# Order of the second-phase products and of the combining in a seven-product matmul block

## The chip, the cores and the metric

The kernel runs on one core of one Trainium2 chip. The metric is the device time of one execution in microseconds (us), as the median of several runs. The core has four engines that matter here, each with its own queue of instructions: TensorE (PE) multiplies, VectorE (DVE) and ScalarE (ACT) do elementwise work, and GpSimd (POOL) and SyncE (SP) issue DMA transfers here.

## What is computed

The reference is a two-layer decoder trunk over 256 tokens of width 2048 in float32. The change lies in the last line of each layer, the gated feed-forward part of width 5632:

```python
for l in range(DEPTH):
    ...
    x = x + mixed @ w_out[l]
    h2 = rms_norm(x, norm2_g[l])
    x = x + (jax.nn.silu(h2 @ w_gate[l]) * (h2 @ w_up[l])) @ w_down[l]
```

## The kernel before

**Tiles.** The 256 tokens are two halves of 128. A weight tile is 256 rows by 512 columns, loaded as 128 x 1024 by one DMA of 512 KB (`raw_load`, L81, seven buffers, issued by SP in program order). Float32 weights are multiplied as a sum of two parts: `split2` (L88) casts the tile on ScalarE to `wh` (L94, five buffers) and subtracts on VectorE to get the rest, `wl` (L95, four buffers). `mm3` (L123) then issues three matmuls of 512 columns: L124 with wh, L125 with wl, L126 with wh again. An ordinary tile (`unit`, L128) takes 12 matmuls, a tile of a seven-product block (`s_unit`, L566) takes 6.

**The feed-forward part.** Its 5632 columns are 11 blocks of 512. For block 0 of each layer, `gate_up` (L646) computes gate and up in the ordinary way. For the ten others, `seven` (L563) takes gate and up of both token halves as a 2 x 2 by 2 x 2 block product, with seven block products in place of eight. The tokens' halves give the left blocks, even and odd groups of rows of the gate and up weights the right ones: B11 and B21 from w_gate, B12 and B22 from w_up.

A seven-product block has two phases, and five PSUM banks (`bank[0]` to `bank[4]`, tiles named m, the pool `pa` with five buffers):

- In the first phase, L583 to L603, each of four steps loads B11, B12 and B22, forms three sums of them on VectorE (L591, L592, L595), and issues five products, into banks 0, 1, 3, 4 and 2. The sum B11 + B12 + B22, tile t2, is used in a product, then a DMA issued by POOL adds B21 to it in place (L597), and it is kept for later.
- Then the banks are combined: m0 is bank 0 plus bank 3 (L607 on ScalarE, L608 on VectorE), c21 is bank 2 plus m0 (L609) and is copied back into bank 2 (L610, ScalarE), c12 is bank 1 plus m0 (L611) plus bank 4 (L613), c22 is bank 1 plus c21 (L612).
- In the second phase, L615 to L622, the four B21 tiles are multiplied into bank 0 and the four kept tiles into bank 2. Banks 0 and 2 then hold the gate of the two token halves, c12 and c22 their up values with the sign turned.
- Last, L623 to L628: silu of banks 0 and 2 on ScalarE (L625), the product with c12 and c22 on VectorE (L627), and `act_later` (L555), which has the result transposed.

**Transposes.** `act_T` (L539) transposes the gated result on TensorE into a PSUM tile `ps_f` of which there is one buffer, casts it on ScalarE (L543) and subtracts on VectorE (L544), to give a pair of tiles aT for the down projection.

**Order.** The seven-product blocks and the ordinary tiles (gate and up of block 0, and all down projections, `std_stream`) are two generators; each `yield` of a seven-product block lets the ordinary stream issue so many tiles that both end together. A clock counts issued tiles (`tick`, L107: 1 for an ordinary tile, 0.5 for a product of a seven-product block), and `later(delay, fn)` (L104) runs a function when the clock has gone on by `delay`. `act_later` asks for the two transposes 2 and 3 ticks later. The framework then puts the instructions of each engine into an order of its own, by the dependences; that order is fixed in the built program. The seam, below, is the place where one seven-product block ends and the next begins.

Of the kernel before, what the change touches and what calls it, by code (L numbers as in the profile page):

```python
# [15 lines left out]
AF = mybir.ActivationFunctionType  # L16
ALU = mybir.AluOpType
# [46 lines left out]
def trunk(ctx, tc, x, xt, w_in, w_out, w_gate, w_up, w_down, sgu_w, sgu_g, consts,  # L64
          band, out):
    nc = tc.nc
# [14 lines left out]
    def raw_load(src, parts=1):  # L81
        raw = wp.tile([P, 2, NB], F32, tag="raw", name="raw", bufs=7)
        n = 2 // parts
        for i in range(parts):
            nc.sync.dma_start(raw[:, i * n : (i + 1) * n, :], src[:, i * n : (i + 1) * n, :])
        return raw

    def split2(raw):  # L88
        wh = wp.tile([P, 2, NB], F32R, tag="wh", name="wh", bufs=5)
        wl = wp.tile([P, 2, NB], F32R, tag="wl", name="wl", bufs=4)  # L90
        step = 2 if clock[0] > 1 else 1
        for j in range(0, 2, step):
            src = raw[:, j : j + step, :]
            nc.scalar.copy(wh[:, j : j + step, :], src)  # L94
            nc.vector.tensor_tensor(  # L95
                wl[:, j : j + step, :], src, f(wh[:, j : j + step, :]), ALU.subtract
            )
        return wh, wl
# [5 lines left out]
    def later(delay, fn):  # L104
        pending.append((clock[0] + delay, next(serial), fn))

    def tick(w=1.0):  # L107
        clock[0] += w
        due = sorted((e for e in pending if e[0] <= clock[0]), key=lambda e: e[:2])
        pending[:] = [e for e in pending if e[0] > clock[0]]  # L110
        for e in due:
            e[2]()
# [10 lines left out]
    def mm3(acc, ah, al, wh, wl, first, last, again=False):  # L123
        nc.tensor.matmul(acc, ah, wh, start=first, stop=False, skip_group_check=again)  # L124
        nc.tensor.matmul(acc, ah, wl, start=False, stop=False, skip_group_check=again)  # L125
        nc.tensor.matmul(acc, al, wh, start=False, stop=last, skip_group_check=again)  # L126
# [70 lines left out]
    def finish_rms(ss, width):  # L197
        tot = small([P, NTOK], "tot")
        nc.vector.tensor_reduce(tot, ss, AX.X, ALU.add)
        r = inv_rms(tot, NTOK, width)  # L200
        return [r[:, t : t + 1] for t in range(NTOK)]
# [38 lines left out]
    for lay in range(L):  # L240
# [287 lines left out]
        rstd2 = finish_rms(ss2, D)  # L528
# [4 lines left out]
        nrstd2 = [nr[:, t : t + 1] for t in range(NTOK)]  # L533
# [16 lines left out]
        def release(live=live, held=held, act_T=act_T):  # L550
            while held and live[0] < ACT_TILES:
                live[0] += 1
                act_T(*held.pop(0))

        def act_later(b, sg, held=held, release=release):  # L555
            for c in range(2):
                def ready(c=c):
                    held.append((b, c, sg))
                    release()

                later(2 + c, ready)

        def seven(b, lay=lay, pairs2=pairs2, ext2=ext2, act_later=act_later):  # L563
            bank = [pa.tile([P, NB], F32, tag="acc", name=f"m{i}") for i in range(5)]

            def s_unit(raw, m, i, op, first, last, bank=bank):  # L566
                wh, wl = split2(raw)
                for j in range(2):
                    ah, al = (op(2 * i + j, h) for h in range(2))
                    mm3(  # L570
                        bank[m], ah, al, wh[:, j, :], wl[:, j, :], first and j == 0,
                        last and j == 1, m in (0, 2),
                    )
                tick(0.5)

            def a_op(k, t):
                return lambda p, h: pairs2[p][:, h, k, t * P : (t + 1) * P]

            def e_op(n):
                return lambda p, h: ext2[p][:, h, n, :]  # L580

            kept = []
            for i in range(4):  # L583
                b11 = raw_load(w_gate[lay, b, i, 0])
                b12 = raw_load(w_up[lay, b, i, 0])
                b22 = raw_load(w_up[lay, b, i, 1])
                t2 = ap.tile([P, 2, NB], F32, tag="spt", name="t2", bufs=4)
                first, last = i == 0, i == 3
                s_unit(b11, 0, i, a_op(0, 0), first, last)
                yield  # L590
                nc.vector.tensor_tensor(b11, b11, b12, ALU.add)  # L591
                nc.vector.tensor_tensor(t2, b11, b22, ALU.add)  # L592
                s_unit(b11, 1, i, e_op(1), first, last)
                yield
                nc.vector.tensor_tensor(b12, b12, b22, ALU.add)  # L595
                s_unit(t2, 3, i, e_op(2), first, last)
                nc.gpsimd.dma_start(t2, w_gate[lay, b, i, 1], accum_op=ALU.add)  # L597
                yield
                s_unit(b22, 4, i, e_op(3), first, last)
                yield  # L600
                s_unit(b12, 2, i, e_op(0), first, last)
                yield
                kept.append(t2)  # L603
            m0, c12, c21, c22 = (
                zp.tile([P, NB], F32, tag="z", name=v) for v in ("m0", "c12", "c21", "c22")
            )
            nc.scalar.copy(m0, bank[0])  # L607
            nc.vector.tensor_tensor(m0, bank[3], m0, ALU.add)  # L608
            nc.vector.tensor_tensor(c21, bank[2], m0, ALU.add)  # L609
            nc.scalar.copy(bank[2], c21)  # L610
            nc.vector.tensor_tensor(c12, bank[1], m0, ALU.add)  # L611
            nc.vector.tensor_tensor(c22, bank[1], c21, ALU.add)  # L612
            nc.vector.tensor_tensor(c12, bank[4], c12, ALU.add)  # L613
            yield
            for i in range(5):  # L615
                if i < 4:
                    b21 = raw_load(w_gate[lay, b, i, 1])
                    s_unit(b21, 0, i, a_op(1, 0), False, i == 3)
                    yield
                if i > 0:  # L620
                    s_unit(kept[i - 1], 2, i - 1, a_op(1, 1), False, i == 4)
                    yield  # L622
            sg = [m0, c21]  # L623
            for t, c in ((0, bank[0]), (1, bank[2])):
                nc.scalar.activation(sg[t], c, AF.Silu, scale=rstd2[t])  # L625
            for t, c in ((0, c12), (1, c22)):
                nc.vector.scalar_tensor_tensor(sg[t], c, nrstd2[t], sg[t], ALU.mult, ALU.mult)  # L627
            act_later(b, sg)  # L628
            yield

        seven_done = [False]
# [1 line left out]
        def s_stream(seven=seven):  # L633
            for b in S_BLOCKS:
                yield from seven(b)
# [171 lines left out]
```

## Time and profile before

| | |
|---|---|
| runs of the kernel (3) | 1949.12 to 1950.69 us, median 1949.98 |
| profiled execution | 1948.9 us |
| its span, first to last instruction | 1947.2 us |
| mean granted TensorE clock | 0.998 |
| matmuls | 8836 |
| read from HBM | 422.66 MB, 218 GB/s over the span |

Rows of groups of instructions give the line, engine, operation, output and input tiles and shapes, the count, busy time and mean duration. Rows of a timeline begin with the start in us from the span's start and the duration, and end in brackets with the idle time of the engine before them and what ended it. Rows of waits give who waited for whom: us in total, how often, and the longest. Rows of stretches (A:B) give their length, the busy time and count of PE, PEld (weight loads of TensorE), DVE, ACT and POOL, the granted clock of TensorE, the busy share of the DMA engines and GB/s. Matmuls are pipelined: the row of one lasts 0.39 us, while in a dense stretch they start 0.227 us apart.

### The profile page before, as it was taken

How to read it: one execution, taken by the hardware profiler on the slowest of the kernel's cores; microseconds unless marked ns; L12 is line 12 of the kernel's file. 1: busy time of each engine (PE TensorE's matmuls, PEld its weight loads, DVE VectorE, ACT ScalarE, POOL GpSimd, SP SyncE). 2: the span in 40 equal slices, each digit the busy share in tenths (PEclk: the TensorE clock that was granted, in tenths of full speed). 3: DMA queues.
4: the chain of work that ended last, by engine and by line, in shares of the span. 5: the costliest groups of instructions: out<-in, count | busy, mean ns of one | idle time of the engine just before them, and what ended most of it. 6: DMA issues, size and time to landing. Idle time of an engine off the chain costs nothing.

```text
span 1947.2 us, 25055 instructions
## 1 busy us (share of the span) xinstructions
PE 1929.0 (99%) x8836; PEld 1577.2 (81%) x8836; DVE 1657.5 (85%) x1752; ACT 1304.9 (67%) x1729; POOL 122.1 (6%) x124
## 2 busy tenths in 40 slices
PE   9999999999999999999999999999999999999999
PEld 7788887878888888888887888878788888888887
DVE  6666689999999999999556666899999999999993
ACT  7566566667767776777756755666677677767675
POOL 1210000000000000000002000000000000000000
PEclk9999999999999999999999999999999999999999
DMA  9544557667777787778555345576678777876783
GB/s 368 190 146 152 185 173 238 219 217 245 253 214 242 243 265 221 236 227 273 195 203 191 126 170 176 174 247 226 201 243 263 222 241 226 271 216 237 237 264 124
DMA packets 118958, 426.41 MB, mean 219 GB/s; under 512 B 13232, under 2 KB 13872, under 8 KB 118832
## 3 DMA queue, kind: packets, MB, share of 16 engines
q1 hardware_dynamic: 105264, 375.52, 53.1%
q0 software_dynamic: 13568, 49.29, 13.6%
q8 instruction: 69, 1.13, 0.2%
q14 instruction: 57, 0.47, 0.1%
HBM read 422.66 MB, written 2.10 MB: 218 GB/s over the span
## 4 chain that ended last, share of the span: by engine, by line
PE 91%; issue 3%; DVE 3%; ACT 2%; POOL 1%; DMA 1%; SPq 0%; ACTq 0%; DVEq 0%; POOLq 0%
PE m L125 13%; PE m L124 13%; PE m L126 13%; PE acc L125 8%; PE acc L126 8%; PE acc L124 8%; PE dacc L124 8%; PE dacc L125 8%; PE dacc L126 8%; PE ps_f L188 1%; DVE wl L95 1%; POOL ir L171 1%; PE ps_v L361 1%; ACT wh L94 1%; PE ps_n L188 1%
## 5 line engine op out<-in xcount | busy, mean ns | idle before, releaser
L94 ACT CAST wh<-raw 128x1024 fp32r<-128x1024 f32 (+1 forms) x786 | 804.2, 1049 | 443.4 <-DVE raw L591 178.0
L95 DVE TENSOR_TENSOR wl<-raw,wh 128x1024 fp32r<-128x1024 f32 (+1 forms) x786 | 934.2, 1218 | 170.9 <-PE acc L125 92.7
L125 PE MATMUL m<-wl,ext 128*128 128x512 f32 x640 | 253.0, 395 | 0.3 <-DVE wl L95 0.2
L124 PE MATMUL m<-wh,ext 128*128 128x512 f32 x640 | 251.8, 395 | 0.7 <-ACT wh L94 0.7
L126 PE MATMUL m<-wh,ext 128*128 128x512 f32 x640 | 250.7, 392 | 0.0
L125 PE MATMUL dacc<-wl,aT 128*128 128x512 f32 x576 | 224.9, 390 | 0.0
L126 PE MATMUL dacc<-wh,aT 128*128 128x512 f32 x576 | 224.5, 390 | 0.0
L124 PE MATMUL dacc<-wh,aT 128*128 128x512 f32 x576 | 222.7, 393 | 1.0 <-ACT wh L94 0.9
L95 DVE TENSOR_TENSOR wl<-t,wh 128x1024 fp32r<-128x1024 f32 x160 | 194.6, 1220 | 2.2 <-issue 1.3
L94 ACT CAST wh<-t 128x1024 fp32r<-128x1024 f32 x160 | 168.5, 1053 | 34.4 <-PE m L126 14.2
L125 PE MATMUL m<-wl,hT 128*128 128x512 f32 x480 | 187.2, 390 | 0.0
L126 PE MATMUL m<-wh,hT 128*128 128x512 f32 x480 | 187.2, 390 | 0.0
L124 PE MATMUL m<-wh,hT 128*128 128x512 f32 x480 | 185.8, 389 | 0.0
L124 PE MATMUL acc<-wh,hT 128*128 128x512 f32 x448 | 179.4, 403 | 0.7 <-ACT wh L94 0.7
L125 PE MATMUL acc<-wl,hT 128*128 128x512 f32 x448 | 176.0, 393 | 1.1 <-DVE wl L95 1.1
L126 PE MATMUL acc<-wh,hT 128*128 128x512 f32 x448 | 175.8, 392 | 0.0
L597 POOL DMA_DIRECT2D t<-in_w_gate_dram x80 | 68.4, 855 | 1331.0 <-DVE wl L95 1188.7
L124 PE MATMUL acc<-wh,aT 128*128 128x512 f32 x384 | 151.6, 395 | 0.0
L126 PE MATMUL acc<-wh,aT 128*128 128x512 f32 x384 | 150.0, 391 | 0.0
L125 PE MATMUL acc<-wl,aT 128*128 128x512 f32 x384 | 149.6, 389 | 0.0
L125 PEld LDWEIGHTS m<-wl,ext 128*128 128x128 f32 x640 | 120.7, 189 | 32.2 <-DVE wl L95 7.9
L124 PEld LDWEIGHTS m<-wh,ext 128*128 128x128 f32 x640 | 120.5, 188 | 27.4 <-ACT wh L94 2.7
(140 smaller groups left out, 2710.1 us busy)
## 6 DMA issues: line engine op xcount, KB each, us to landing
raw<-in_w_gate_dram SPq DMA_DIRECT2D x176, 512.0 KB, 5.6
raw<-in_w_up_dram SPq DMA_DIRECT2D x176, 512.0 KB, 5.4
raw<-in_w_down_dram SPq DMA_DIRECT2D x176, 512.0 KB, 4.3
raw<-in_w_in_dram SPq DMA_DIRECT2D x108, 512.0 KB, 4.2
t<-in_w_gate_dram POOLq DMA_DIRECT2D x80, 512.0 KB, 5.8
raw<-in_w_out_dram SPq DMA_DIRECT2D x64, 512.0 KB, 3.3
bias<-in_band_dram POOLq DMA_DIRECT2D x8, 512.0 KB, 4.5
xr<-in_xt_dram SPq DMA_DIRECT2D x8, 256.0 KB, 5.8
```

What stands on the lines that cost most here:

```text
L94: nc.scalar.copy(wh[:, j : j + step, :], src)
L95: nc.vector.tensor_tensor(wl[:, j : j + step, :], src, f(wh[:, j : j + step, :]), ALU.subtract)
L124: nc.tensor.matmul(acc, ah, wh, start=first, stop=False, skip_group_check=again)
L125: nc.tensor.matmul(acc, ah, wl, start=False, stop=False, skip_group_check=again)
L126: nc.tensor.matmul(acc, al, wh, start=False, stop=last, skip_group_check=again)
L171: anchor[0] = nc.gpsimd.tensor_tensor(r, ms, mhalf[:, :n], ALU.pow)
L188: nc.tensor.transpose(ps[:, j, t * P : (t + 1) * P], blocks[t][:, j * P : (j + 1) * P], ident)
L361: nc.tensor.matmul(pv[:, r, i], pt[:, (r * n + i) * (t + 1) + b, :], zkv[b][:, cols], start=b == 0, stop=b == t,)
L597: nc.gpsimd.dma_start(t2, w_gate[lay, b, i, 1], accum_op=ALU.add)
```

## The change

The combining is cut into steps that are given out between the products of the second phase; all four B21 products come first, then the four kept ones; silu and multiplication of bank 0 are given out after the sixth product, those of bank 2 through `later(1, ...)`, that is one tick after the block's last product.

```diff
             nc.scalar.copy(m0, bank[0])
             nc.vector.tensor_tensor(m0, bank[3], m0, ALU.add)
-            nc.vector.tensor_tensor(c21, bank[2], m0, ALU.add)
-            nc.scalar.copy(bank[2], c21)
-            nc.vector.tensor_tensor(c12, bank[1], m0, ALU.add)
-            nc.vector.tensor_tensor(c22, bank[1], c21, ALU.add)
-            nc.vector.tensor_tensor(c12, bank[4], c12, ALU.add)
             yield
-            for i in range(5):
+
+            def add(out, x, y):
+                nc.vector.tensor_tensor(out, x, y, ALU.add)
+
+            def gated(t, psum, sg, c):
+                nc.scalar.activation(sg, psum, AF.Silu, scale=rstd2[t])
+                nc.vector.scalar_tensor_tensor(sg, c, nrstd2[t], sg, ALU.mult, ALU.mult)
+
+            steps = {
+                0: lambda: add(c21, bank[2], m0),
+                1: lambda: (nc.scalar.copy(bank[2], c21), add(c12, bank[1], m0)),
+                2: lambda: (add(c22, bank[1], c21), add(c12, bank[4], c12)),
+                5: lambda: gated(0, bank[0], m0, c12),
+            }
+            for i in range(8):
                 if i < 4:
-                    b21 = raw_load(w_gate[lay, b, i, 1])
-                    s_unit(b21, 0, i, a_op(1, 0), False, i == 3)
-                    yield
-                if i > 0:
-                    s_unit(kept[i - 1], 2, i - 1, a_op(1, 1), False, i == 4)
-                    yield
-            sg = [m0, c21]
-            for t, c in ((0, bank[0]), (1, bank[2])):
-                nc.scalar.activation(sg[t], c, AF.Silu, scale=rstd2[t])
-            for t, c in ((0, c12), (1, c22)):
-                nc.vector.scalar_tensor_tensor(sg[t], c, nrstd2[t], sg[t], ALU.mult, ALU.mult)
-            act_later(b, sg)
+                    s_unit(raw_load(w_gate[lay, b, i, 1]), 0, i, a_op(1, 0), False, i == 3)
+                else:
+                    s_unit(kept[i - 4], 2, i - 4, a_op(1, 1), False, i == 7)
+                yield
+                steps.get(i, lambda: None)()
+            later(1, lambda: gated(1, bank[2], c21, c22))
+            act_later(b, [m0, c21])
             yield
```

## The prediction

> **What bounds the kernel now.** I read the page's busy times first, then who TensorE waited for, then stretches of the run.
>
> ```profile
> PE 1929.0 (99%) x8836; PEld 1577.2 (81%) x8836; DVE 1657.5 (85%) x1752; ACT 1304.9 (67%) x1729; POOL 122.1 (6%) x124
> PE ps_f L188 <- DVE aT L544: 3.1, 2, 1.5
> PE dacc L124 <- ACT wh L94: 0.9, 2, 0.4
> PE m L124 <- ACT wh L94: 0.7, 2, 0.3
> 423.00:600.00 177.00, 176.94 (x788) 145.32 (x787) 170.86 (x161) 122.16 (x142) 10.26 (x12) 1.00 0.77 244
> ```
>
> TensorE is busy 99% of the span and the change takes no matmul from it. The waits (us, times, longest) say how little there is to win: among the weights' products of the gate, up and down stage (tiles m and dacc, and the transposes ps_f), the three largest waits of TensorE for another engine are 4.7 us in all, 3.1 of them in two waits of ps_f. The stretch 423 to 600 has 788 matmuls without a hole. VectorE, 170.9 us of the same 177, is nearly as full, so a change in its order could cost something; that has to be looked at as well.
>
> The place of both ps_f waits is the seam between the second and the third seven-product block, once in each layer. Engine by engine:
>
> ```profile
> 413.48 0.39 PE L126 MATMUL m<-wh,hT 128*128 128x512 f32 x1
> 413.71 0.39 PE L124 MATMUL m<-wh,hT 128*128 128x512 f32 x1
> 413.94 0.60 PE L188 MATMUL ps_f<-ident,sg 128*128 128x128 f32 x4
> ...
> 415.31 0.40 PE L126 MATMUL m<-wh,hT 128*128 128x512 f32 x1
> 417.23 0.33 PE L188 MATMUL ps_f<-ident,m 128*128 128x128 f32 x1 [1.53 <-DVE aT L544]
> ...
> 417.77 0.50 PE L124 MATMUL m<-wh,ext 128*128 128x512 f32 x1
> 418.71 1.12 PE L124 MATMUL dacc<-wh,aT 128*128 128x512 f32 x2 [0.45 <-ACT wh L94]
> 419.63 0.66 PE L125 MATMUL m<-wl,ext 128*128 128x512 f32 x1
> ...
> 421.80 0.61 PE L125 MATMUL dacc<-wl,aT 128*128 128x512 f32 x1
> ...
> 422.49 0.40 PE L125 MATMUL dacc<-wl,aT 128*128 128x512 f32 x1
> ```
> ```profile
> 413.97 0.69 ACT L625 ACTIVATE c<-m,ir 128x512 f32<-128x512 f32 x1 [2.09 <-PE m L126]
> 414.57 0.59 ACT L543 CAST aT<-ps_f 128x512 fp32r<-128x512 f32 x1
> 416.67 2.00 ACT L94 CAST wh<-raw 128x1024 fp32r<-128x1024 f32 x2 [1.51 <-DVE raw L591]
> ```
> ```profile
> 414.69 0.75 DVE L627 SCALAR_TENSOR_TENSOR c<-c,nr,c 128x512 f32<-128x512 f32 x1 [0.73 <-ACT c L625]
> 415.36 1.22 DVE L591 TENSOR_TENSOR raw<-raw 128x1024 f32<-128x1024 f32 x1
> 416.50 0.68 DVE L544 TENSOR_TENSOR aT<-ps_f,aT 128x512 fp32r<-128x512 f32 x1
> 417.10 1.22 DVE L592 TENSOR_TENSOR t<-raw 128x1024 f32<-128x1024 f32 x1
> 418.23 2.35 DVE L95 TENSOR_TENSOR wl<-raw,wh 128x1024 fp32r<-128x1024 f32 x2
> ```
>
> The last product on bank 2 starts at 413.48. Its silu (413.97) waits for it on ScalarE; the multiplication L627 waits for the silu on VectorE; behind that stand the addition L591, the copy L544 that frees the one ps_f buffer, L592 and the subtraction that the next matmul (419.63) needs. TensorE, due at 415.54 (415.31 and one start distance of 0.227, from 413.71 less 413.48), goes on at 417.23. And it goes on slowly:
>
> ```profile
> 415.44:418.86 3.42, 1.45 (x8) 0.75 (x7) 3.42 (x5) 2.19 (x3) 0.00 (x0) 1.00 0.00 0
> 418.86:422.27 3.41, 3.41 (x9) 2.44 (x10) 3.41 (x5) 3.36 (x5) 0.00 (x0) 0.50 0.53 167
> 1388.24:1391.66 3.42, 3.42 (x9) 2.46 (x10) 3.42 (x5) 3.37 (x5) 0.00 (x0) 0.50 0.53 174
> 87.76:91.18 3.42, 1.57 (x7) 0.94 (x5) 3.42 (x6) 0.20 (x1) 1.61 (x2) 1.00 0.50 175
> 91.18:94.59 3.41, 2.96 (x17) 2.54 (x18) 2.36 (x5) 3.41 (x12) 0.00 (x0) 1.00 0.61 198
> ```
>
> The granted clock (third column from the end) is 0.50 for 3.41 us after a stretch with 1.45 us of TensorE time, and again at 1388 in layer 2. After a stretch with 1.57 (87.76 to 91.18) it stayed at 1.00.
>
> **The change part by part.** No instruction is added or removed; the built programs have equally many on each engine. What moves:
>
> *Additions and the copy into bank 2 (L609 to L613).* Four additions stood together; now up to three stand behind one or two subtractions more.
>
> ```profile
> 530.19 0.68 DVE L609 TENSOR_TENSOR c<-m,m 128x512 f32<-128x512 f32 x1
> ...
> 531.98 0.68 DVE L613 TENSOR_TENSOR c<-m,c 128x512 f32<-128x512 f32 x1
> 532.58 1.22 DVE L95 TENSOR_TENSOR wl<-raw,wh 128x1024 fp32r<-128x1024 f32 x1
> 534.20 0.39 PE L125 MATMUL m<-wl,hT 128*128 128x512 f32 x1
> ```
>
> They take 0.60 us each (530.19 to 531.98 is three). The subtraction behind them ends at 533.80, its matmul starts at 534.20: 0.40 us to spare, no wait. With three additions behind it the reserve is 0.4 + 1.8 = 2.2 us. A reserve gains nothing where nobody waited: 0. The copy L610 gates the first product on bank 2, which moves from third to fifth place: 0.
>
> *Order of the eight products.* The same 48 matmuls: 0 for TensorE. The loads keep their order on SP, but the third and fourth B21 tiles are wanted earlier by one and two products, 6 and 12 starts of 0.227: 1.36 and 2.72 us. The tightest fourth tile I found:
>
> ```profile
> 590.28 0.33 SPq L85 DMA_DIRECT2D raw<-in_w_gate_dram  x1
> DMA to landing us min/median/max: 6.5/6.5/6.5
> 599.80 1.06 ACT L94 CAST wh<-raw 128x1024 fp32r<-128x1024 f32 x1 [0.94 <-PE m L126]
> DMA to landing us min/median/max: 3.0/4.7/11.2
> ```
>
> It lands at 596.8 and is cast at 599.80: 3.0 us early, so 0.3 is left. I take 0; the other end, if landings lengthen towards the 11.2 us that the second row gives as the longest of all these loads, is the losing rival below. The kept tiles are held longer, until the last four products; their buffers are wanted again by the additions L592 of the next block, which follow its first product: 0. On POOL nothing moves.
>
> *Silu and multiplication of bank 0.* Given out after the sixth product, two after its last. In the built order the multiplication stands two to four subtractions earlier on VectorE, 0.6 us of work out of the seam, put among the kept products, where the reserve is smallest at this same seam.
>
> ```profile
> 409.21 2.36 DVE L95 TENSOR_TENSOR wl<-t,wh 128x1024 fp32r<-128x1024 f32 x2
> 411.22 0.39 PE L125 MATMUL m<-wl,hT 128*128 128x512 f32 x1
> ```
>
> The first of the two subtractions ends 1.22 us after 409.21, and its matmul starts at 411.22: 0.8 us to spare, of which 0.2 is left. Bank 0 comes free sooner for the next block: 0, since it waited for nothing.
>
> *Silu and multiplication of bank 2, one tick later.* On VectorE the multiplication stands at most one subtraction later, and the transposes of its result are due next.
>
> ```profile
> 356.95 0.74 DVE L627 SCALAR_TENSOR_TENSOR c<-c,nr,c 128x512 f32<-128x512 f32 x1
> 360.05 0.27 PE L188 MATMUL ps_f<-ident,m 128*128 128x128 f32 x1
> ```
>
> At the first seam it ends at 357.69, 2.36 us ahead of them; one subtraction more, 1.22 us, would still fit. Behind it on ScalarE stand the next block's casts, up to three further on by then, and the next block's bank 2 is first written by its fifth product, four products or 5.4 us on: 0.
>
> *The seam at 413.* In the built order ScalarE still has the bank 2 silu right ahead of the aT copy L543: that wait stays. VectorE, though, has L591 and the next L544 and L592 ahead of bank 2's multiplication. Step by step: one matmul of the next block now stands ahead of the last bank 2 product, which so starts at 413.71; silu 0.49 after it (as 413.97 after 413.48), 414.20; L543 0.60 later, 414.80 to 415.39; L544, not behind a multiplication or L591 any more, 415.42 to 416.10; the transposes at 416.15 instead of 417.23. Then L592 at 416.02, the subtraction at 417.15 to 418.37, its matmul at 418.55 instead of 419.63. Three transposes, which stood ahead of it, now follow (0.11 each), and the multiplication takes 0.67 us of VectorE (414.69 to 415.36) ahead of the next subtraction, which ends at 420.15. So the dacc matmul of 421.80 starts at 420.20, and the one of 422.49, two starts further, at 420.66: 1.8 us earlier. Of it 0.5 is the shorter wait: at full clock the old order would have had five starts from 419.63, so 420.77. The other 1.3 is the slow clock, if that goes. I take it as gone: in my steps the stretch 415.44 to 418.86 holds 0.3 + 0.6 + 0.6 + 0.3 = 1.8 us of TensorE time (tails of 0.39 counted as the rows do), above the 1.57 that kept its clock.
>
> [...]
>
> **Sum.** Two seams, 1.8 us each: 3.6. The profiled execution took 1948.9 us (span 1947.2, 1.7 around it): 1945.3. The median of the runs, 1949.98, is 1.1 above it, so for the runs 1946.4, 0.18% less.
>
> **The rivals.**
> *The clock halves again.* The seam gives its 0.5 twice: 1949.0. For it: a halving was seen after 1.45 us and none after 1.57, my 1.8 is an estimate from steps that can each be 0.2 off, and the stretches need not fall on the same places of the run. Against: both observed stretches, on their side.
> *The stall goes altogether.* From 415.31 to 422.49 are 7.2 us, for 11 starts of 0.227 and four transposes of 0.11, 2.9 us: 4.2 lost per layer. Both back: 1949.98 less 8.5 is 1941.5. Against: the silu of bank 2 still stands ahead of the aT copy.
> *Slower: the B21 tiles come late.* Four loads are now used up in a row. Where landings lengthen by over the 0.3 us left at the tightest block, ScalarE stands at the cast with everything behind it, the subtraction follows, and once VectorE's reserve is eaten TensorE waits. A mean of 0.4 us in each of 20 blocks is 8 us: 1946.4 + 8 = 1954.4. For it: the 11.2 us landing. Against: the reserve of 2.2 us worked out above, and landings of 6.5 at the tightest.
> *It does nothing at the seam* falls in with the first rival.
>
> **How the numbers follow.** Forecast 0.45, clock halved again 0.25, stall gone 0.12, tiles late 0.18. 0.2% (3.9 us), about what a measurement of this kernel can tell from no change, puts the line for faster at 1946.1, close to the forecast, whose own range is 1944.9 to 1947.9 (0.4 a matmul or cast either way at each step of two seams). Some 0.19 of its 0.45 lies below the line: faster 0.19 + 0.12 = 0.31, same 0.26 + 0.25 = 0.51, slower 0.18. The range takes in the first two rivals and leaves out the third: 1941.5 to 1951.0.
>
> **What would show it.** Right: at 413 to 423 the ps_f wait for L544 falls from 1.5 to about 0.6 us, VectorE has L591 and L592 ahead of bank 2's multiplication, and both stretches with a clock of 0.50 are gone. Clock wrong: the stall shorter, but a 0.50 left. Tiles late: waits of wh for the w_gate loads, which the waits before do not have in this stage, and TensorE waiting for wh in the eight products. I am wrong altogether if TensorE's waits grow at seams that had none.

## The result and the profile after

| kernel | runs | median us | lowest to highest |
|---|---|---|---|
| before, run beside it | 16 | 1950.05 | 1947.38 to 1951.55 |
| changed | 16 | 1946.72 | 1944.41 to 1949.65 |

The ratio is 0.9983, with a 95% interval of 0.9976 to 0.999: some 3.3 us less. The forecast was 1946.4 us. The profiled execution took 1945.63 us, with a span of 1943.8 (before: 1948.9 and 1947.2).

The busy times of the changed kernel, and TensorE's waits in the gate, up and down stage (us in total, times, longest):

```profile
PE 1927.5 (99%) x8836; PEld 1579.1 (81%) x8836; DVE 1660.9 (85%) x1752; ACT 1301.5 (67%) x1729; POOL 123.2 (6%) x124
...
PE ps_f L188 <- DVE aT L544: 0.9, 2, 0.4
PE dacc L124 <- ACT wh L94: 0.9, 2, 0.4
PE m L124 <- ACT wh L94: 0.7, 2, 0.3
PE m L125 <- DVE wl L95: 0.6, 2, 0.3
```

The counts are those of before. The two ps_f waits have gone from 3.1 us to 0.9; the two pairs of waits for wh are unchanged; those of m L125 for wl are 0.6 us in two, where there was one of 0.2. The waits of ps_f, dacc L124 and m L125 lie at the two seams; those of m L124 lie ahead of them (290 to 410 and 1268 to 1380 us), before and after. TensorE at the seam of layer 1, from the timeline of the changed kernel:

```profile
414.86 0.40 PE L126 MATMUL m<-wh,hT 128*128 128x512 f32 x1
415.69 0.33 PE L188 MATMUL ps_f<-ident,m 128*128 128x128 f32 x1 [0.44 <-DVE aT L544]
415.96 0.50 PE L124 MATMUL m<-wh,ext 128*128 128x512 f32 x1
416.90 0.73 PE L124 MATMUL dacc<-wh,aT 128*128 128x512 f32 x2 [0.44 <-ACT wh L94]
417.96 0.55 PE L125 MATMUL m<-wl,ext 128*128 128x512 f32 x1 [0.32 <-DVE wl L95]
...
420.51 0.78 PE L125 MATMUL dacc<-wl,aT 128*128 128x512 f32 x1
...
421.51 0.49 PE L125 MATMUL dacc<-wl,aT 128*128 128x512 f32 x1
```

ScalarE and then VectorE at the same place (L615 and L616 are here the silu and its multiplication, L625 and L627 before):

```profile
413.75 0.69 ACT L615 ACTIVATE c<-m,ir 128x512 f32<-128x512 f32 x1 [3.52 <-PE m L126]
414.34 0.58 ACT L543 CAST aT<-ps_f 128x512 fp32r<-128x512 f32 x1
```
```profile
413.55 1.22 DVE L591 TENSOR_TENSOR raw<-raw 128x1024 f32<-128x1024 f32 x1
414.95 0.69 DVE L544 TENSOR_TENSOR aT<-ps_f,aT 128x512 fp32r<-128x512 f32 x1 [0.18 <-ACT aT L543]
415.56 1.22 DVE L592 TENSOR_TENSOR t<-raw 128x1024 f32<-128x1024 f32 x1
416.69 1.22 DVE L95 TENSOR_TENSOR wl<-raw,wh 128x1024 fp32r<-128x1024 f32 x1
417.82 0.75 DVE L616 SCALAR_TENSOR_TENSOR c<-c,nr,c 128x512 f32<-128x512 f32 x1
```

Before, VectorE stood idle for bank 2's silu and had the multiplication and L591 ahead of the copy L544. Now L591 is done in the time of that idling, L544 follows its cast at once, and the multiplication comes behind L592 and a subtraction, where it holds up only the next subtraction. The transposes still wait, 0.83 us after the last product (415.69 less 414.86) where it was 1.92.

From the last product ahead of the stall to the second dacc matmul with wl it is 6.65 us (421.51 less 414.86) where it was 7.18 (422.49 less 415.31): 0.53 less. The same in layer 2, before and then after:

```profile
1384.70 0.40 PE L126 MATMUL m<-wh,hT 128*128 128x512 f32 x1
...
1391.88 0.39 PE L125 MATMUL dacc<-wl,aT 128*128 128x512 f32 x1
```
```profile
1383.18 0.40 PE L126 MATMUL m<-wh,hT 128*128 128x512 f32 x1
...
1388.08 0.50 PE L125 MATMUL dacc<-wl,aT 128*128 128x512 f32 x1
...
1388.65 0.40 PE L125 MATMUL dacc<-wl,aT 128*128 128x512 f32 x1
```

Here it is 5.47 us where it was 7.18: 1.71 less. The difference between the seams is the clock. These are stretches of the changed kernel (the granted clock is the third column from the end):

```profile
414.87:418.28 3.41, 2.21 (x7) 0.92 (x6) 3.33 (x4) 3.41 (x5) 0.00 (x0) 1.00 0.00 0
418.28:421.70 3.42, 3.42 (x11) 2.71 (x10) 2.75 (x4) 2.22 (x4) 0.00 (x0) 0.50 0.69 223
1380.84:1384.25 3.41, 2.97 (x16) 2.06 (x14) 3.20 (x4) 2.17 (x4) 0.00 (x0) 1.00 0.00 0
1384.25:1387.66 3.41, 2.65 (x11) 1.60 (x11) 3.41 (x4) 3.41 (x4) 0.00 (x0) 1.00 0.13 40
```

In layer 1 the clock is halved to 0.50 for one stretch of 3.42 us, in layer 2 it stays at 1.00. Together the seams give 0.53 + 1.71 = 2.24 of the 3.4 us between the two spans. The rest is spread over the run (0.45 ahead of the first walk, 0.54 between the two, 0.17 behind the second) and isn't shown to be the change's: executions of one kernel differ by more than that (1947.38 to 1951.55 us of the kernel before).

### The profile page after: what moved, and what is told of

It is laid out like the page before. It is cut to its first block, busy times and chain, and to the rows that moved or that the text cites. A ratio compares the mean times of both kernels' runs of the same rounds, so it can differ in the third digit from the quotient of the medians.

```text
span 1943.8 us, 25047 instructions
## 1 busy us (share of the span) xinstructions
PE 1927.5 (99%) x8836; PEld 1579.1 (81%) x8836; DVE 1660.9 (85%) x1752; ACT 1301.5 (67%) x1729; POOL 123.2 (6%) x124
## 4 chain that ended last, share of the span: by engine, by line
PE 92%; issue 3%; DVE 2%; ACT 1%; POOL 1%; DMA 1%; SPq 0%; ACTq 0%; DVEq 0%; POOLq 0%
PE m L125 13%; PE m L124 13%; PE m L126 13%; PE acc L125 8%; PE acc L126 8%; PE acc L124 8%; PE dacc L125 8%; PE dacc L124 8%; PE dacc L126 8%; PE ps_f L188 1%; POOL ir L171 1%; PE ps_v L361 1%; DVE wl L95 1%; PE ps_n L188 1%; ACT s L338 0%
## 5 line engine op out<-in xcount | busy, mean ns | idle before, releaser
L124 PE MATMUL m<-wh,ext 128*128 128x512 f32 x640 | 252.6, 396 | 0.7 <-ACT wh L94 0.7
L125 PE MATMUL m<-wl,ext 128*128 128x512 f32 x640 | 252.3, 394 | 0.7 <-DVE wl L95 0.6
L124 PE MATMUL dacc<-wh,aT 128*128 128x512 f32 x576 | 224.9, 391 | 0.9 <-ACT wh L94 0.9
L125 PE MATMUL dacc<-wl,aT 128*128 128x512 f32 x576 | 225.1, 391 | 0.0
L125 PE MATMUL m<-wl,hT 128*128 128x512 f32 x480 | 187.4, 390 | 0.0
L124 PE MATMUL m<-wh,hT 128*128 128x512 f32 x480 | 186.7, 390 | 0.0
L124 PE MATMUL acc<-wh,hT 128*128 128x512 f32 x448 | 179.6, 403 | 1.1 <-ACT wh L94 1.1
L125 PE MATMUL acc<-wl,hT 128*128 128x512 f32 x448 | 176.1, 393 | 0.9 <-DVE wl L95 0.9
L124 PE MATMUL acc<-wh,aT 128*128 128x512 f32 x384 | 151.8, 395 | 0.0
L125 PE MATMUL acc<-wl,aT 128*128 128x512 f32 x384 | 149.8, 390 | 0.0
L125 PEld LDWEIGHTS m<-wl,ext 128*128 128x128 f32 x640 | 120.5, 188 | 32.2 <-DVE wl L95 8.1
L124 PEld LDWEIGHTS m<-wh,ext 128*128 128x128 f32 x640 | 120.5, 188 | 27.1 <-ACT wh L94 2.8
```

## The experiments

Each was timed in five rounds beside the kernel before.

| label | kernel | median us | before us | ratio (95% interval) |
|---|---|---|---|---|
| e_order | before, new product order alone | 1945.99 | 1949.24 | 0.9982 (0.9973 to 0.9991) |
| e_spread | before, combining spread alone | 1948.55 | 1949.24 | 0.9997 (0.9988 to 1.0006) |
| e_later | before, bank 2's silu a tick later alone | 1949.49 | 1949.24 | 1.0 (0.9992 to 1.0009) |
| e_nolater | changed, without that tick | 1947.05 | 1949.24 | 0.9991 (0.9982 to 0.9999) |
| e_before_apart | before, block 0's transposes moved | 1944.87 | 1948.84 | 0.998 (0.9971 to 0.9989) |
| e_after_apart | changed, the same move | 1945.25 | 1948.84 | 0.9982 (0.9973 to 0.9991) |
| e_order_apart | new order alone, the same move | 1944.64 | 1950.04 | 0.9979 (0.997 to 0.9988) |
| e_before_raw6 | before, six load buffers | 1971.54 | 1948.84 | 1.0123 (1.0108 to 1.0139) |
| e_after_raw6 | changed, six load buffers | 1978.76 | 1948.84 | 1.0154 (1.014 to 1.0168) |
| e_before_adds | before, one addition issued three times | 1956.48 | 1950.04 | 1.0039 (1.0026 to 1.0051) |
| e_after_adds | changed, one addition issued three times | 1951.39 | 1950.04 | 1.0011 (1.0002 to 1.002) |

### Which part of the change earns it

The first kernel has the order of the eight products alone; combining, silu and multiplication stay where they were.

```diff
-            for i in range(5):
-                if i < 4:
-                    b21 = raw_load(w_gate[lay, b, i, 1])
-                    s_unit(b21, 0, i, a_op(1, 0), False, i == 3)
-                    yield
-                if i > 0:
-                    s_unit(kept[i - 1], 2, i - 1, a_op(1, 1), False, i == 4)
-                    yield
+            for i in range(8):
+                if i < 4:
+                    s_unit(raw_load(w_gate[lay, b, i, 1]), 0, i, a_op(1, 0), False, i == 3)
+                else:
+                    s_unit(kept[i - 4], 2, i - 4, a_op(1, 1), False, i == 7)
+                yield
```

> The kernel before with the order of the products alone changed: four B21 products, then four kept ones; additions, silus and multiplications given out where they were. Theory (the gain lies at the two seams and comes from what stands ahead of bank 2's multiplication on VectorE): in the built order L591 now stands ahead of that multiplication and the transposes come behind five more matmuls, so the ps_f wait of 1.5 us goes, some 1.4 us of stall per seam are left of 2.75, and the time is that of the changed kernel or up to 2 us less: 1944 to 1947. Rival (spreading the additions gives VectorE room everywhere): 1950, no gain. Rival (early silu of bank 0, late silu of bank 2): 1950, no gain.

It has the whole gain: 3.25 us of medians against the change's 3.3. Its seam is built in another way than the change's. TensorE, then VectorE (L625 is the multiplication here):

```profile
415.77 0.40 PE L126 MATMUL m<-wh,hT 128*128 128x512 f32 x1
416.87 0.50 PE L124 MATMUL m<-wh,ext 128*128 128x512 f32 x1 [0.70 <-ACT wh L94]
417.82 0.73 PE L124 MATMUL dacc<-wh,aT 128*128 128x512 f32 x2 [0.45 <-ACT wh L94]
...
419.94 0.27 PE L188 MATMUL ps_f<-ident,m 128*128 128x128 f32 x1
...
420.97 0.40 PE L125 MATMUL dacc<-wl,aT 128*128 128x512 f32 x1
```
```profile
414.46 1.22 DVE L591 TENSOR_TENSOR raw<-raw 128x1024 f32<-128x1024 f32 x1
415.60 0.74 DVE L625 SCALAR_TENSOR_TENSOR c<-c,nr,c 128x512 f32<-128x512 f32 x1
416.26 1.22 DVE L592 TENSOR_TENSOR t<-raw 128x1024 f32<-128x1024 f32 x1
417.40 1.22 DVE L95 TENSOR_TENSOR wl<-raw,wh 128x1024 fp32r<-128x1024 f32 x1
418.53 0.68 DVE L544 TENSOR_TENSOR aT<-ps_f,aT 128x512 fp32r<-128x512 f32 x1
```

The four transposes stand behind the first matmuls of the next block (419.94), so nothing at the stall waits for ps_f; what TensorE waits for is the cast of the next block's first sum. The order of products shifts what is due when, and the built order of TensorE changes with it. From 415.77 to 420.97 are 5.2 us where the kernel before took 7.18.

The next two leave the order of products as it was. One spreads the five additions and the copy behind the first three products:

```diff
-            nc.vector.tensor_tensor(c21, bank[2], m0, ALU.add)
-            nc.scalar.copy(bank[2], c21)
...
+            steps = {
+                0: lambda: (add(c21, bank[2], m0), nc.scalar.copy(bank[2], c21)),
+                1: lambda: add(c12, bank[1], m0),
+                2: lambda: (add(c22, bank[1], c21), add(c12, bank[4], c12)),
+            }
...
                     s_unit(b21, 0, i, a_op(1, 0), False, i == 3)
                     yield
+                    steps.get(i, lambda: None)()
```

> The kernel before with the additions alone spread between the first three B21 products, the old order of products and the silus at the end. Theory: the seam's built order is that of before, so 1950 within 1 us, with the ps_f wait of 1.5 us twice and the two slow-clock stretches. Rival (room on VectorE): 1946 to 1948. Rival (silus): 1950.

the other gives out bank 2's silu and multiplication one tick later:

```diff
-            for t, c in ((0, bank[0]), (1, bank[2])):
-                nc.scalar.activation(sg[t], c, AF.Silu, scale=rstd2[t])
...
+            gated(0, bank[0], m0, c12)
+            later(1, lambda: gated(1, bank[2], c21, c22))
```

> The kernel before with the silu and multiplication of bank 2 alone given out one tick later. Theory: the built order still has bank 2's multiplication ahead of L591 and L544 at the seam, so 1950 within 1 us. Rival (room on VectorE): 1950. Rival (late silu of bank 2 unblocks ScalarE): 1946 to 1948.

Both stay at the time of before, 0.7 us below it and 0.3 above, with intervals that take in no change, and the seam is that of before. This is the wait in the spread kernel's timeline, and in the other one's list of waits:

```profile
418.46 0.33 PE L188 MATMUL ps_f<-ident,m 128*128 128x128 f32 x1 [1.52 <-DVE aT L544]
```
```profile
PE ps_f L188 <- DVE aT L544: 3.1, 2, 1.5
```

The fourth is the changed kernel without the tick:

```diff
-            later(1, lambda: gated(1, bank[2], c21, c22))
+            gated(1, bank[2], c21, c22)
```

> The changed kernel with bank 2's silu and multiplication given out right at the block's end, not one tick later. Theory: what counts is the order of the products, so the seam is as in the kernel with the order alone, 1944 to 1947. Rival (late silu of bank 2): back to 1949 or 1950. Rival (room on VectorE): as the changed kernel, 1947.

Its median of 1947.05 lies 0.05 us above what was expected, and its gain is only just clear of none (0.9982 to 0.9999). Its seam is built like that of e_order, without a ps_f wait and with one of 0.70 us for the cast of the next block's first sum, as there. So the one-tick delay isn't what frees L544. It decides only in which of two ways the seam is relieved, and no difference between the two can be measured. The early silu of bank 0 was not run alone; as the order alone has the whole gain, nothing measurable is left for it.

### Is the seam all there is to it

If the change is worth only what it does at the seams, it must be worth nothing in a kernel whose seams don't collide. The collision was taken away in another place: `gate_up`, the ordinary block 0, asks for its transposes (ps_f from sg) 0.5 and 1.5 ticks after its end, in place of 2 and 3.

```diff
-        def act_later(b, sg, held=held, release=release):
+        def act_later(b, sg, first=2, held=held, release=release):
...
-                later(2 + c, ready)
+                later(first + c, ready)
...
-            act_later(b, sg)
+            act_later(b, sg, 0.5)
```

> The kernel before, with gate_up's transposes asked for 0.5 and 1.5 ticks after its end in place of 2 and 3, so that they no longer fall on the seam between the second and third seven-product block. Theory (all that the change gives is at these two seams): both seam stalls and both slow-clock stretches go, 2 times 3.9 us, so 1941 to 1943, and TensorE waits nowhere for ps_f. Rival (the change gives room on VectorE everywhere): the same here; it shows in the next run.

> The changed kernel with the same shift of gate_up's transposes. Theory: with the collision gone the change is worth nothing any more: within 0.1% of the kernel before with that shift, 1941 to 1943. Rival (room on VectorE everywhere): 2 to 3 us below it, 1938 to 1940. Rival (B21 tiles late): above it by 1 us or more.

Without the collision the kernels stand at 1944.87 and 1945.25: the change is worth nothing there, as expected. But both were expected at 1941 to 1943, by 3.9 us a seam, and stayed 1.9 and 2.3 us above the upper end of that. The ps_f stall and the halved clock at the seams are gone from the profile of e_before_apart (no ps_f row among TensorE's waits, a mean clock of 1.0); in their place TensorE waits some 20 and 40 us further on, where the kernel before had no wait:

```profile
437.78 0.50 PE L125 MATMUL m<-wl,ext 128*128 128x512 f32 x1 [0.36 <-DVE wl L95]
...
459.10 0.50 PE L124 MATMUL m<-wh,ext 128*128 128x512 f32 x1 [0.34 <-ACT wh L94]
```

In the kernel before VectorE works 170.9 of 177 us in this stage (423 to 600). The reading that fits: while TensorE stood at the seam, VectorE got ahead; with TensorE going on, VectorE and the casts behind it are late a little further on, first with a subtraction, then with a cast. What VectorE does there was not altered in a run of its own, so this is argued. The gaps between starts at 437 and 459, above the usual 0.227, add up to some 1.3 us. In both layers together the waits of m L125 for wl are 0.7 us in two, and those of m L124 for wh 1.3 in four, where the kernel before has 0.2 in one and 0.7 in two.

The move on top of the new order alone:

> The kernel before with both edits that pay alone: the order of the products, and gate_up's transposes away from the seam. Theory (both take away the same stall): no sum of the gains, 1944 to 1946. Rival (order pays elsewhere too): 1941 to 1943.

1944.64: the two reliefs don't add up, as expected, since they relieve one place. Its ratio is 0.9979 where the change has 0.9983, with intervals that overlap, so it isn't shown to beat the change; it beats the kernel before.

### What four loads in a row cost

The losing rival said that the B21 tiles come late. The changed kernel's list of waits has a row that the one of before lacks, and an example of it is this fourth B21 tile, issued at 394.25 (landing times in the second line) and cast late:

```profile
ACT wh L94 <- DMA raw<-in_w_gate_dram: 6.7, 6, 2.1
...
394.25 0.33 SPq L85 DMA_DIRECT2D raw<-in_w_gate_dram  x1
DMA to landing us min/median/max: 5.5/5.5/5.5
...
399.86 1.06 ACT L94 CAST wh<-raw 128x1024 fp32r<-128x1024 f32 x1 [0.56 <-DMA raw<-in_w_gate_dram]
```

So ScalarE does wait, six times, but TensorE's waits for wh in this stage haven't grown. To see what is under that reserve, both kernels were run with one load buffer fewer:

```diff
-... name="raw", bufs=7)
+... name="raw", bufs=6)
```

> The kernel before with six buffers for loaded tiles in place of seven, so each load starts one freed buffer later, some 1.3 to 2.7 us. Its fourth B21 tiles land 3.0 to 5.3 us ahead of their cast, so they stay in time; some tiles of the down projection that land 0.1 to 1 us ahead come late. Theory: a few us slower, 1950 to 1956.

> The changed kernel with six buffers. Its fourth B21 tiles land 0.1 to 1.9 us ahead of their cast with seven; with six they come 1 to 2.5 us late in most blocks, against a reserve on VectorE of 0.9 to 3.3 us. Theory (the price of four loads in a row is real and hidden by a thin reserve): it loses more by the sixth buffer than the kernel before does, 5 to 15 us more. Rival (loads are not near the limit): both lose the same, within 2 us.

The kernel before loses 22.7 us, far above what was expected of it; the changed one loses 32.0 (1978.76 less 1946.72), 9.3 more, by four executions of each. ScalarE's waits for loads, in the kernel before and then in the changed one, both with six buffers:

```profile
ACT wh L94 <- DMA raw<-in_w_down_dram: 35.0, 20, 6.9
...
ACT wh L94 <- DMA raw<-in_w_gate_dram: 13.2, 13, 1.8
```
```profile
ACT wh L94 <- DMA raw<-in_w_down_dram: 44.6, 22, 7.1
...
ACT wh L94 <- DMA raw<-in_w_gate_dram: 21.4, 19, 3.0
```

That the changed kernel needs the seventh buffer more is shown, since nothing else was altered; that the 9.3 us are the price of four B21 loads in a row is not. The waits for tiles of the down projection grow as much as those for gate tiles, and TensorE's waits for casts in the down projection (dacc L124) fall from 6.6 to 4.6 us. What grows is the ps_f wait, from 3.1 us in two to 11.2 in eight, the longest 2.5, and at 499 a down tile comes 2.8 us late:

```profile
PE ps_f L188 <- DVE aT L544: 11.2, 8, 2.5
...
499.36 1.05 ACT L94 CAST wh<-raw 128x1024 fp32r<-128x1024 f32 x1 [2.80 <-DMA raw<-in_w_down_dram]
```

The reading that fits: the cast holds up a subtraction, the subtraction the copy L544, and that the transposes, the stall of the seam at another block. These rows don't show that chain step by step. The profiled execution of the changed kernel with six buffers also has the lower mean clock, 0.996 where that of the kernel before with six has 0.999. Whether the four gate loads push the down tile back stays open, as does how near the changed kernel with seven buffers stands to such a loss.

### What spreading the additions is worth

The addition c22 = bank 1 + c21 is issued three times in each seven-product block, which adds two VectorE instructions of 0.60 us in each of 20 blocks.

```diff
             nc.vector.tensor_tensor(c22, bank[1], c21, ALU.add)
+            nc.vector.tensor_tensor(c22, bank[1], c21, ALU.add)
+            nc.vector.tensor_tensor(c22, bank[1], c21, ALU.add)
```

> The kernel before with the addition c22 issued three times in place of once: two more of 0.6 us each in the group of additions, 1.2 us of VectorE per block, same result. Theory (the reserve behind that group is 0.4 us in the tight blocks): TensorE waits some 0.8 us behind the group in blocks with a reserve under 1.2, about half of the 20, so 6 to 12 us more: 1955 to 1961. Rival (VectorE's reserve is ample, being made up soon): 1949 to 1951.

> The changed kernel with the same two more additions. Theory (the spread adds 1.8 us of reserve there, hidden as long as nobody waits): no wait behind the additions, 0 to 4 us more for the work itself further on: 1947 to 1951, so the change is worth more here, 6 to 10 us, than it is without. Rival (a reserve is a reserve, in total the same work): the same loss as the kernel before.

The kernel before loses 6.4 us, as expected; the changed one 4.7, 0.4 above the upper end of what was expected. In the kernel before, the additions now hold up the subtraction behind them (537.73 to 538.94), which had 0.4 us to spare. VectorE, and the matmul that starts when the subtraction ends:

```profile
537.73 1.21 DVE L95 TENSOR_TENSOR wl<-raw,wh 128x1024 fp32r<-128x1024 f32 x1
```
```profile
538.53 0.39 PE L124 MATMUL m<-wh,hT 128*128 128x512 f32 x1
539.00 0.50 PE L125 MATMUL dacc<-wl,aT 128*128 128x512 f32 x1
```

The start at 539.00 is 0.47 after the one before it, 0.24 over the usual distance. In the changed kernel TensorE's waits for a subtraction in this stage are hardly longer (m L125 for wl 0.7 us in two, 0.6 in two without the added work), but the added work shows up elsewhere, as waits for casts that were 0.7 us in two without it:

```profile
PE m L124 <- ACT wh L94: 3.8, 6, 1.1
```

By the medians the change is worth 5.1 us here and 3.3 without the added work; 6 to 10 were expected. The 1.8 between them, of 24 us of added work, are within the scatter of the runs, and the changed kernel differs in the order and the silus too. So it is argued from the traces, and not shown, that the spreading enlarges the reserve behind the additions. In the kernel as it is that reserve is not used, and the spread kernel above shows its value there: none that can be measured.

## Why the prediction was right

**The seam, step by step.** The walk can be laid over the profile, as distances from the start of the last product ahead of the stall (415.31 in the prediction, 414.86 in the profile after; layer 2 from 1383.18):

| step | predicted | layer 1 | layer 2 |
|---|---|---|---|
| copy L544 starts | 0.11 | 0.09 | 0.09 |
| first transpose | 0.84 | 0.83 | 0.84 |
| subtraction starts | 1.84 | 1.83 | 1.83 |
| its matmul | 3.24 | 3.10 | 3.10 |
| first dacc matmul with wl | 4.89 | 5.65 | 4.90 |
| second dacc matmul with wl | 5.35 | 6.65 | 5.47 |

The first column is the prediction's times less 415.31 (415.42, 416.15, 417.15, 418.55, 420.20, 420.66). Up to the halving in layer 1, and throughout in layer 2, each step lies within 0.14 us. Where the clock stays whole the seam gives 1.71 for the 1.8 forecast; where it is halved, 0.53 for the 0.5. The mechanism as forecast (L591 and L544 ahead of bank 2's multiplication) is what the changed kernel shows.

**The clock: the step that failed.** The prediction took both halvings as gone, since its stretch would hold 1.8 us of TensorE time, above the 1.57 that had kept the clock. In layer 1 the stretch held 2.21 us, and the clock was halved all the same. TensorE's time in the stretch doesn't settle it: the same 3.41 us behind the last product hold 2.21 us in layer 2 as well,

```profile
1383.18:1386.59 3.41, 2.21 (x7) 0.92 (x6) 3.32 (x4) 3.41 (x5) 0.00 (x0) 1.00 0.00 0
```

without a halving. What differs between the layers is where the stall falls. In the trace of before the two halved stretches start 969.38 us apart (1388.24 less 418.86), and the two stalls 969.39 (1384.70 less 415.31). In the changed kernel the stalls are 968.32 us apart (1383.18 less 414.86). Carried over to it, the spacing of 969.38 puts 1384.25 in layer 2 where layer 1 has 414.87, the start of the 3.41 us ahead of the halving. Those 3.41 us hold the stall of layer 1 (2.21 us of rows), while the stall of layer 2 starts ahead of 1384.25 and is shared by the 3.41 us on either side (2.97 and 2.65). To carry the spacing over is the author's estimate: no run shows that the clock goes by it.

Why did a stretch with 1.57 us keep its clock and one with 2.21 not? The time of rows is not work: behind a wait a row here lasts 0.50 us (1384.29 and 1386.28 in the changed kernel), in a dense stretch 0.39, while starts are 0.227 apart. Counted by starts, at 0.227 us a product and 0.11 a transpose, 415.44 to 418.86 of before holds some 0.9 us and 414.87 to 418.28 of the changed kernel some 1.2 (five products, the first from 414.86, and one transpose); a halving follows both. The stretch from 87.76 of before holds some 1.4 (six products and the end of one), and 415.44 to 418.86 of e_order, at its seam, some 1.4 as well, in 2.16 us of rows:

```profile
415.44:418.86 3.42, 2.16 (x8) 0.92 (x7) 3.42 (x5) 3.28 (x5) 0.00 (x0) 1.00 0.00 0
```

Both keep their clock; in e_order the products behind the seam start 0.23 to 0.24 us apart (419.00 to 419.71). The counts are estimates from the rows, and they don't decide alone: the 3.41 us from 1383.18 in layer 2 hold some 1.2 too, without a halving. How the clock is decided no run shows. The prediction set rows against rows: by the same count its stretch with 1.8 us, the end of one product, one transpose and four products, holds some 1.1, less than the 1.2 that a halving followed in layer 1.

So neither the forecast nor its first rival holds for every execution. The executions can be sorted by their mean granted clock; a halved stretch of 3.41 us takes 0.0009 off that mean (half of 3.41, of 1947):

| mean clock | before: executions, median us | changed: executions, median us |
|---|---|---|
| 1.0 | none | 6, 1944.82 |
| 0.999 | 17, 1947.72 | 3, 1946.45 |
| 0.998 | 39, 1949.23 | 7, 1947.80 |
| 0.997 and 0.996 | 19, 1950.5 and 1951.4 | none |

(The 75 of before are those beside three groups of experiments.) A mean of 1.0 leaves no room for a halved stretch, so six of the sixteen executions of the changed kernel had none, as forecast; its profiled execution, at 0.999, had the one in layer 1. Below 1.0 the mean doesn't say where the clock was halved: the profile of e_later, at 0.997, has a halved stretch in the attention stage (93.89 to 97.30, below), away from the seams. With that reserve, at the same mean clock the change is worth 1.3 to 1.4 us, near the 2 x 0.5 of the shorter waits, and an estimated 1.9 of the 3.3 us come from fewer halvings, where the prediction's sum had 1.0 and 2.6. That its median came out within 0.3 us of the measured one is in part luck: the middle of a mixture, and not a proof that the halvings go.

**The parts costed at nothing.** Right for two, by the runs that did them alone: spreading (0.9997) and the tick (1.0) move nothing that can be measured. The early silu of bank 0 was not run alone. The loads were costed at nothing with 0.3 us left at the tightest tile; that much was not left, since six casts wait for gate tiles, the longest 2.1 us, but TensorE doesn't wait for them. What the prediction didn't say is which edit earns the gain: it costed the new order of products at 0 for itself and took the seam as a joint outcome. The order alone earns it.

**The rivals.** That the tiles come late was right in its first step, with ScalarE waiting in six casts, and wrong in the next: TensorE doesn't wait for them. The 9.3 us with six buffers are another quantity than the 8 of this rival, and come by another way. That the stall goes altogether was set at 4.2 us a layer: e_before_apart, without the stall, loses some 1.3 of that again further on, by the gaps in layer 1. Its 1944.87, and not 1941.5, is what that end was worth here.

## What to carry to other kernels

A change that gives out work in another order may earn its gain through what the built order of the engines does at one place: look there in the timeline of each part done alone before crediting an edit. Where a second engine is busy 97% of the time, a stall of the bounding engine may be worth less than its length: here some 1.3 of an estimated 4.2 us came back as waits further on. When executions spread by more than the change, sort them by the granted clock, but look in the trace for where the clock was halved before putting it down to the change. And count work by starts of matmuls: rows behind a wait are longer, here 0.50 us where dense ones last 0.39.

## What the hardware showed that was not expected

- A clock halved to 0.50 for 3.41 us after 3.41 us with 2.21 us of TensorE rows, some 1.2 us of work by starts, and in six of sixteen executions of that kernel a mean clock of 1.0, with no room for a halving.
- One halving can come at a quite different place: in the profile of e_later the clock is also halved in the attention stage of layer 1, which the profile of before doesn't show (its clock is 1.00 from 0 to 300):

```profile
90.48:93.89 3.41, 1.34 (x10) 1.14 (x10) 3.41 (x6) 2.00 (x9) 1.61 (x2) 1.00 0.64 203
93.89:97.30 3.41, 3.41 (x12) 2.74 (x10) 0.56 (x3) 2.07 (x5) 0.00 (x0) 0.50 0.80 256
```

- One load buffer of seven taken away costs 22.7 us, 1.2%, in a kernel whose ScalarE with seven waits for no gate tile, and for two down tiles 1.9 us in all.
